# The first stage of a four-branch layer with two input blocks loaded first and its norm and transposes taken by half blocks

## The chip, the cores and the metric

The kernel runs on one core of a Trainium2 chip. The metric is device time in microseconds (us) for one execution of the whole kernel. Five engines run programs of their own and meet at semaphores: TensorE (PE; its weight loads are PEld), VectorE (DVE), ScalarE (ACT), GpSimd (POOL) and SyncE (SP), which only issues transfers. Each engine takes its instructions in the order in which they stand in its program.

## The reference, cut to what matters

```python
def hybrid_layer(x, norm_g, w_in, ...):
    h = rms_norm(x, norm_g)            # x: (1, 512, 1024)
    proj = h @ w_in                    # w_in: (1024, 11208)
    (a_u, a_v, a_z, b_q, b_c, b_qi, b_ki, b_wi, b_z, c_b, c_c, c_x, c_z,
     d_q, d_k, d_v, d_f, d_z, gates) = jnp.split(proj, points, axis=-1)
    y_a = chunked_spatial_gating(a_u, a_v, ...) * jax.nn.silu(a_z)
    y_b = dsa_attention(b_q, b_c, b_qi, b_ki, b_wi, ...) * jax.nn.silu(b_z)
    y_c = short_gated_conv(c_b, c_c, c_x, conv_w) * jax.nn.silu(c_z)
    y_d = forgetting_attention(d_q, d_k, d_v, d_f, fox_b_f) * jax.nn.silu(d_z)
    branch_d = jnp.einsum('nbsw,nwd->bsnd', jnp.stack([y_a, y_b, y_c, y_d]), w_branch)
    merged = jnp.sum(jax.nn.sigmoid(gates) * branch_d, axis=2)
    return x + merged @ w_out          # then a last rms_norm
```

`rms_norm` divides a row of `x` by the root of its mean square and multiplies it by `norm_g`. Everything else in the layer needs the normed input, and the part at issue here is that norm and the first projection, `d_v` (512 columns of `w_in`).

## The kernel before, in words

Every matmul operand is kept as two parts, a rounded high part and the rest as low part, and a product is three matmuls: high with high, high with low, low with high. ACT writes the high part (L80), DVE the low part (L81); the helper `split` does both.

The first stage works on four blocks t of 128 rows of `x` (`xt`, 128x1024). For a block, `norm_x` squares and sums it on ACT (L223), scales the sum on DVE (`rs_v`, L95), takes the root on POOL (`rs`, L96), and multiplies `xt` by the root and by `gB` on DVE in two halves of 512 columns (`xs`, L228). `gB` is `norm_g` on all partitions: two one-row matmuls (`gp`, L263) spread it, and DVE copies them out (L264). `transposed_x` turns the block on PE, four 128x128 transposes to a half (`pt`, L237), and splits each half into `hh` and `hl`, which hold the normed input, turned, for the whole program. `dv_split(i)` splits a quarter of the `d_v` weights (`dvwh`, `dvwl`), and `dv_product(t, i)` is six matmuls of block t with quarter i into `ps_dv` (L144 to L146). The results of the four blocks are split to `vfh`, `vfl`.

All of this stands under `in_order()`, which ties the instructions of PE, DVE and ACT to the order in which the code gives them. What follows (`vfh`/`vfl`, and the next projections with their weights `rawc`, `rawi`, `raw`) is outside it; a scheduler places it among the first stage's instructions when the program is built. The loads of `x`, `norm_g` and the weights are all issued by SP, in the code's order. The remaining stages (the attention branches with a top-k on DVE, the conv, the gates, the output) are some thirty further projections by `proj_fm` with work of the branches between them.

Below, "pt(t, h)" stands for the four transposes of half h of block t, and "hh(t, h)", "hl(t, h)", "xs(t, h)" for the split and the scaling of that half.

Of the kernel before, what the change touches and what calls it, by code (L numbers as in the profile page):

```python
# [8 lines left out]
F32 = mybir.dt.float32  # L9
F32R = mybir.dt.float32r  # L10
AF = mybir.ActivationFunctionType
ALU = mybir.AluOpType
# [5 lines left out]
P = 128  # L18
S = 512
D = 1024  # L20
W = 512
NT = S // P
NK = D // P
# [10 lines left out]
def hybrid_kernel(ctx: ExitStack, tc, x, norm_g, w_in, gm_ln_g, gm_ln_b, gm_w_s, gm_b_s,  # L34
                  dsa_kv_g, dsa_w_uk, dsa_w_uv, conv_w, fox_b_f, w_branch, w_out, final_g, out):
    nc = tc.nc
# [5 lines left out]
    hh = act.tile([P, NK, S], F32R, name="hh")  # L42
    hl = act.tile([P, NK, S], F32R, name="hl")
# [7 lines left out]
    def big(name, dtype=F32R, shape=(P, 4, 512)):  # L51
        return sb.tile(list(shape), dtype, tag="big", name=name, bufs=8)
# [13 lines left out]
    def small(name, cols=1, bufs=4):  # L66
        return sb.tile([P, cols], F32, tag=name, name=name, bufs=bufs)
# [9 lines left out]
    def split(hi, lo, src, scale=None, eng=nc.vector):  # L77

        if scale is None:
            nc.scalar.activation(hi, src, AF.Copy)  # L80
            eng.tensor_tensor(lo, src, hi.bitcast(F32), op=ALU.subtract)  # L81
        else:
            nc.scalar.activation(hi, src, AF.Copy, scale=scale)
            nc.vector.scalar_tensor_tensor(lo, src, scale, hi.bitcast(F32),
                                           op0=ALU.mult, op1=ALU.subtract)
# [6 lines left out]
    def rsqrt(dst, src, scale, n=1):  # L92

        v = small("rs_v", n) if n == 1 else small("rs_w", n, 1)
        nc.vector.tensor_scalar(v, src, scale, EPS, op0=ALU.mult, op1=ALU.add)  # L95
        nc.gpsimd.tensor_tensor(dst, v, negh[:, 0:n], op=ALU.pow)  # L96
# [46 lines left out]
    def term_tm(ps, ah, al, wh, wl, k):  # L143
        nc.tensor.matmul(ps, ah, wh, start=(k == 0), stop=False)  # L144
        nc.tensor.matmul(ps, ah, wl, start=False, stop=False)  # L145
        nc.tensor.matmul(ps, al, wh, start=False, stop=(k == NK - 1))  # L146
# [34 lines left out]
    gB = big("gB", F32, (P, D))  # L181
# [3 lines left out]
    def load_x(t):  # L185
        nc.sync.dma_start(xts[t // 2][:, t % 2, :], x[t * P:(t + 1) * P, :])
# [3 lines left out]
                          w_in[i * 256:(i + 1) * 256, D_V:D_V + W].rearrange("(k p) c -> p k c", p=P))  # L190

    g1 = big("g1", F32, (1, D))
    load_x(0)
    nc.sync.dma_start(g1, norm_g)
    load_dv(0)
    load_x(1)
    load_dv(1)
    load_dv(2)
    load_dv(3)
# [16 lines left out]
    nc.vector.tensor_copy(up, upf)  # L216


    def norm_x(t):
        xt = xts[t // 2][:, t % 2, :]  # L220
        xs = xs2[t // 2][:, t % 2, :]
        ss = small("ss")
        nc.scalar.activation(xs, xt, AF.Square, accum_out=ss)  # L223
        rs = small("rs")
        rsqrt(rs, ss, 1.0 / D)
        for half in range(2):
            hs = slice(half * 512, half * 512 + 512)
            nc.vector.scalar_tensor_tensor(xs[:, hs], xt[:, hs], rs, gB[:, hs],  # L228
                                           op0=ALU.mult, op1=ALU.mult)
        return xs  # L230

    def transposed_x(t, xs):
        for half in range(2):
            pt = at.tile([P, 4, P], F32, tag="at", name="pt")
            for j in range(4):
                k = half * 4 + j
                nc.tensor.transpose(pt[:, j, :], xs[:, k * P:(k + 1) * P], ident)  # L237
            split(hh[:, half * 4:half * 4 + 4, t * P:(t + 1) * P],
                  hl[:, half * 4:half * 4 + 4, t * P:(t + 1) * P], pt)

    def dv_split(i):
        js = slice((i % 2) * 2, (i % 2) * 2 + 2)
        wh, wl = dvw[i // 2]
        split(wh[:, js, :], wl[:, js, :], dvr[i // 2][:, js, :])

    ps_dv = [mm.tile([P, W], F32, tag="mm", name="ps_dv") for _ in range(NT)]

    def dv_product(t, i):
        ts_ = slice(t * P, (t + 1) * P)
        for k in (2 * i, 2 * i + 1):  # L250
            wh, wl = dvw[k // 4]
            term_tm(ps_dv[t], hh[:, k, ts_], hl[:, k, ts_], wh[:, k % 4, :], wl[:, k % 4, :], k)

    with in_order():

        warm = psum("warm")
        for _ in range(8):
            nc.tensor.transpose(warm[:, 0:P], ident, ident)

        for half in range(2):  # L260
            gs = slice(half * 512, half * 512 + 512)
            gp = psum("gp")
            nc.tensor.matmul(gp, up[0:1, 0:P].bitcast(F32), g1[:, gs], start=True, stop=True)  # L263
            nc.vector.tensor_copy(gB[:, gs], gp)  # L264
        xs = norm_x(0)
        dv_split(0)
        transposed_x(0, xs)
        xs = norm_x(1)
        dv_product(0, 0)
        dv_split(1)  # L270
        transposed_x(1, xs)
        dv_product(0, 1)
        dv_product(1, 0)
        dv_product(1, 1)
        dv_split(2)
        xs = norm_x(2)
        dv_split(3)
        dv_product(0, 2)
        dv_product(1, 2)
        transposed_x(2, xs)  # L280
        xs = norm_x(3)
        dv_product(0, 3)
        dv_product(1, 3)
        dv_product(2, 0)
        dv_product(2, 1)
        transposed_x(3, xs)
        dv_product(2, 2)
        dv_product(2, 3)
        for i in range(4):
            dv_product(3, i)  # L290
    vfh, vfl = pair("vf")
    for t in range(NT):
        split(vfh[:, t, :], vfl[:, t, :], ps_dv[t])
# [301 lines left out]
    for t in range(NT):  # L595
# [9 lines left out]
        rs = small("rs")  # L605
# [264 lines left out]
```

## Time and profile before

| | |
|---|---|
| three runs | 709.07, 710.71, 711.07 us (median 710.71) |
| profiled execution, its own time | 711.89 us |
| its span in the trace | 710.2 us |
| PE busy | 693.9 us |
| DVE busy | 364.5 us |
| ACT busy | 275.1 us |

The span runs from the first to the last instruction of the trace; the execution's own time is 1.7 us longer. In a row of the timeline stand the start, the duration, the engine, the line, the operation and its tiles, the count of instructions merged in it, and in brackets how long the engine was idle before it and what ended the wait. A matmul's duration includes its way through the array, so successive matmuls overlap; the distance of their starts is what one costs.

### The profile page before, as it was taken

What the parts mean: (1) busy time and instruction counts of PE and PEld (TensorE: products, weight loads), DVE (VectorE), ACT (ScalarE), POOL (GpSimd) and SP (SyncE); (2) the same over time, 40 slices, a digit from 0 to 9 for tenths busy, and PEclk for the clock granted to TensorE, in tenths of its full rate; (3) what the DMA queues carried; (4) which work ended last, traced back from release to release, by engine and by line L of the source; (5) the groups of instructions that cost most, each with busy time, mean ns of one, the idle gap of its engine ahead of it and who ended that gap; (6) DMA issues with size and microseconds to landing.
All of it is one profiled execution on the core that took longest, in us unless ns stands there. A gap on an engine that the chain in (4) does not pass through costs nothing.

```text
span 710.2 us, 8000 instructions
## 1 busy us (share of the span) xinstructions
PE 693.9 (98%) x3139; PEld 566.4 (80%) x3139; DVE 364.5 (51%) x638; ACT 275.1 (39%) x439; POOL 169.9 (24%) x110
## 2 busy tenths in 40 slices
PE   7999999988999999999999999999999999999996
PEld 4878767766888888888888888888888888888885
DVE  5825699999953664634233343323522334343454
ACT  4616354354444556433322242223322223333233
POOL 1000487341333323203000021222211132111101
PEclk9999999999999999999999999999999999999999
DMA  6715031312112111242322331322313313133233
GB/s 237 219 64 153 4 118 59 112 59 69 60 60 90 60 60 60 61 147 73 105 83 96 118 114 65 119 77 102 120 60 118 117 61 119 60 118 119 62 117 119
DMA packets 56817, 68.05 MB, mean 96 GB/s; under 512 B 3582, under 2 KB 45067, under 8 KB 56780
## 3 DMA queue, kind: packets, MB, share of 16 engines
q1 hardware_dynamic: 55900, 65.46, 28.3%
q0 software_dynamic: 304, 1.05, 0.4%
q10 hardware_dynamic: 576, 1.05, 0.4%
q8 instruction: 24, 0.39, 0.2%
q14 instruction: 13, 0.11, 0.0%
HBM read 64.80 MB, written 2.10 MB: 94 GB/s over the span
## 4 chain that ended last, share of the span: by engine, by line
PE 85%; DVE 11%; DMA 2%; issue 1%; ACT 0%; SPq 0%; POOLq 0%; POOL 0%; DVEq 0%
PE ps_fm L119 18%; PE ps_fm L120 18%; PE ps_fm L124 18%; PE pb L744 4%; PE pb L745 4%; PE pb L747 4%; DVE sc L474 3%; DVE m L473 2%; PE ps_o L144 2%; PE ps_o L146 2%; PE ps_o L145 2%; DVE sc L466 1%; PE pt_ps L533 1%; PE ps_dv L144 1%; DVE l L511 1%
## 5 line engine op out<-in xcount | busy, mean ns | idle before, releaser
L119 PE MATMUL ps_fm<-hh,wh 128*128 128x512 f32 (+1 forms) x640 | 251.3, 393 | 0.0
L120 PE MATMUL ps_fm<-hl,wh 128*128 128x512 f32 (+1 forms) x640 | 250.0, 391 | 0.0
L124 PE MATMUL ps_fm<-hh,wl 128*128 128x512 f32 (+1 forms) x640 | 162.5, 391 | 0.0
L119 PEld LDWEIGHTS ps_fm<-hh,wh 128*128 128x128 f32 (+1 forms) x640 | 120.1, 188 | 26.0 <-issue 0.9
L120 PEld LDWEIGHTS ps_fm<-hl,wh 128*128 128x128 f32 (+1 forms) x640 | 120.0, 187 | 24.9 <-issue 0.2
L124 PEld LDWEIGHTS ps_fm<-hh,wl 128*128 128x128 f32 (+1 forms) x640 | 119.0, 187 | 25.0 <-issue 0.2
L80 ACT ACTIVATE wh<-raw 128x1024 fp32r<-128x1024 f32 x78 | 82.3, 1056 | 114.1 <-PE ps_fm L120 85.0
L81 DVE TENSOR_TENSOR wl<-raw,wh 128x1024 fp32r<-128x1024 f32 x50 | 61.0, 1222 | 78.4 <-PE ps_fm L124 67.1
L81 POOL TENSOR_TENSOR wl<-raw,wh 128x1024 fp32r<-128x1024 f32 x28 | 69.1, 2474 | 111.9 <-PE ps_fm L124 49.2
L753 POOL TENSOR_TENSOR acc<-acc,sg 128x512 f32<-128x512 f32 x24 | 41.8, 1742 | 155.9 <-DVE sg L752 155.9
L744 PE MATMUL pb<-yh,wh 128*128 128x512 f32 x128 | 49.8, 389 | 0.0
L745 PE MATMUL pb<-yl,wh 128*128 128x512 f32 x128 | 49.8, 389 | 0.0
L81 DVE TENSOR_TENSOR wl<-rawb,wh 128x1024 fp32r<-128x1024 f32 x16 | 19.6, 1225 | 51.3 <-PE ps_fm L124 36.8
L80 ACT ACTIVATE wh<-rawb 128x1024 fp32r<-128x1024 f32 x16 | 16.9, 1057 | 50.6 <-PE ps_fm L120 50.6
L752 DVE TENSOR_TENSOR sg<-pb,sg 128x512 f32<-128x512 f32 x24 | 16.6, 692 | 36.3 <-PE pb L747 36.3
L747 PE MATMUL pb<-yh,wl 128*128 128x512 f32 x128 | 34.2, 389 | 0.0
L519 ACT ACTIVATE l<-l,nm 128x128 f32<-128x128 f32 (+3 forms) x32 | 17.9, 560 | 28.5 <-DVE nm L517 28.5
L771 ACT ACTIVATE sg<-ps_fm 128x512 f32<-128x512 f32 x32 | 19.2, 600 | 24.4 <-PE ps_fm L124 24.4
L747 PEld LDWEIGHTS pb<-yh,wl 128*128 128x128 f32 x128 | 24.0, 188 | 5.0
L744 PEld LDWEIGHTS pb<-yh,wh 128*128 128x128 f32 x128 | 24.0, 188 | 5.0
L745 PEld LDWEIGHTS pb<-yl,wh 128*128 128x128 f32 x128 | 24.0, 188 | 5.0
L145 PE MATMUL ps_o<-wl,mh 128*128 128x512 f32 (+1 forms) x72 | 26.2, 366 | 0.0
(242 smaller groups left out, 913.9 us busy)
## 6 DMA issues: line engine op xcount, KB each, us to landing
raw<-in_w_in_dram SPq DMA_DIRECT2D x39, 1024.0 KB, 4.9
rawb<-in_w_branch_dram SPq DMA_DIRECT2D x8, 1024.0 KB, 4.9
rawt<-in_w_out_dram SPq DMA_DIRECT2D x4, 1024.0 KB, 4.9
xt<-in_x_dram SPq DMA_DIRECT2D x4, 512.0 KB, 8.3
rawt<-in_w_in_dram SPq DMA_DIRECT2D x4, 512.0 KB, 8.4
rawt<-in_w_in_dram SPq DMA_DIRECT2D x2, 1024.0 KB, 5.7
xr<-in_x_dram SPq DMA_DIRECT2D x2, 1024.0 KB, 4.9
out_dram<-o SPq DMA_DIRECT2D x4, 256.0 KB, 2.1
```

What stands on the lines that cost most here:

```text
L80: nc.scalar.activation(hi, src, AF.Copy)
L81: eng.tensor_tensor(lo, src, hi.bitcast(F32), op=ALU.subtract)
L119: nc.tensor.matmul(ps[:m], wh[:, k, :], hh[:, k, :], start=(k == 0), stop=False)
L120: nc.tensor.matmul(ps[:m], wh[:, k, :], hl[:, k, :], start=False, stop=False)
L124: nc.tensor.matmul(ps[:m], wl[:, k, :], hh[:, k, :], start=False, stop=(k == NK - 1))
L144: nc.tensor.matmul(ps, ah, wh, start=(k == 0), stop=False)
L145: nc.tensor.matmul(ps, ah, wl, start=False, stop=False)
L474: nc.vector.match_replace(out=scs[i], in_to_replace=m8, in_values=scs[i], imm_value=TAKEN)
L744: nc.tensor.matmul(pb, bh[:, k, cs_], yh[:, k, :], start=(k == 0), stop=False)
L745: nc.tensor.matmul(pb, bh[:, k, cs_], yl[:, k, :], start=False, stop=False)
L747: nc.tensor.matmul(pb, bl[:, k, cs_], yh[:, k, :], start=False, stop=(k == NH - 1))
L753: nc.gpsimd.tensor_tensor(acc, acc, sg, op=ALU.add)
```

## The change

The load of `norm_g` moves from SP to ACT's queue, ahead of everything on ACT. On SP the first two blocks of `x` come first, then the four quarters of the `d_v` weights, then blocks 2 and 3. The eight transposes on `ident` at the start (`warm`) go; three 512-column matmuls on `up` (`keep_warm(3)`) are put between block 0 and block 1. The norm is cut into `square`, `root` and `scaled` (a half), the turn into `transposed_x` (a half) and `parts_x` (the high or the low part of a half), and all are called in a new order. A product takes the high weights of its two k first and the low weights last.

```diff
     g1 = big("g1", F32, (1, D))
+    nc.scalar.dma_start(g1, norm_g)
     load_x(0)
-    nc.sync.dma_start(g1, norm_g)
+    load_x(1)
     load_dv(0)
-    load_x(1)
     load_dv(1)
...
-    def norm_x(t):
...
+    def square(t):
+        sums[t] = small("ss")
+        nc.scalar.activation(xs2[t // 2][:, t % 2, :], xts[t // 2][:, t % 2, :], AF.Square,
+                             accum_out=sums[t])
+
+    def root(t):
+        roots[t] = small("rs")
+        rsqrt(roots[t], sums[t], 1.0 / D)
+
+    def scaled(t, half):
+        hs = slice(half * 512, half * 512 + 512)
+        nc.vector.scalar_tensor_tensor(xs2[t // 2][:, t % 2, hs], xts[t // 2][:, t % 2, hs], roots[t],
+                                       gB[:, hs], op0=ALU.mult, op1=ALU.mult)
...
+    def transposed_x(t, half):
         xs = xs2[t // 2][:, t % 2, :]
...
+        pt = at.tile([P, 4, P], F32, tag="at", name="pt")
+        for j in range(4):
+            k = half * 4 + j
+            nc.tensor.transpose(pt[:, j, :], xs[:, k * P:(k + 1) * P], ident)
+        pts_x[t, half] = pt
+
+    def parts_x(t, half, part):
+        hi = hh[:, half * 4:half * 4 + 4, t * P:(t + 1) * P]
+        lo = hl[:, half * 4:half * 4 + 4, t * P:(t + 1) * P]
+        if part == 0:
+            nc.scalar.activation(hi, pts_x[t, half], AF.Copy)
+        else:
+            nc.vector.tensor_tensor(lo, pts_x[t, half], hi.bitcast(F32), op=ALU.subtract)
...
-            term_tm(ps_dv[t], hh[:, k, ts_], hl[:, k, ts_], wh[:, k % 4, :], wl[:, k % 4, :], k)
+            nc.tensor.matmul(ps_dv[t], hh[:, k, ts_], wh[:, k % 4, :], start=(k == 0), stop=False)
+            nc.tensor.matmul(ps_dv[t], hl[:, k, ts_], wh[:, k % 4, :], start=False, stop=False)
+        for k in (2 * i, 2 * i + 1):
+            wh, wl = dvw[k // 4]
+            nc.tensor.matmul(ps_dv[t], hh[:, k, ts_], wl[:, k % 4, :], start=False,
+                             stop=(k == NK - 1))
 
     with in_order():
 
         warm = psum("warm")
-        for _ in range(8):
-            nc.tensor.transpose(warm[:, 0:P], ident, ident)
-
+
+        def keep_warm(n):
+            for _ in range(n):
+                nc.tensor.matmul(warm, up[:, 0:P], up, start=True, stop=True)
...
+        square(0)
+        root(0)
+        square(1)
+        for half in range(2):
+            nc.vector.tensor_copy(gB[:, half * 512:half * 512 + 512], gps[half])
+            scaled(0, half)
+            transposed_x(0, half)
+            parts_x(0, half, 0)
+        root(1)
+        parts_x(0, 0, 1)
+        parts_x(0, 1, 1)
+        keep_warm(3)
+        dv_split(0, 0)
+        for half in range(2):
+            scaled(1, half)
+            transposed_x(1, half)
+            parts_x(1, half, 0)
+        dv_split(0, 1)
         dv_product(0, 0)
...
+        parts_x(1, 0, 1)
+        parts_x(1, 1, 1)
         dv_product(1, 0)
...
+        for i in range(1, 4):
+            dv_split(i, 0)
+            dv_split(i, 1)
+            dv_product(0, i)
+            dv_product(1, i)
+            if i > 1:
+                square(i)
+                root(i)
+        for t in (2, 3):
+            for half in range(2):
+                scaled(t, half)
+                transposed_x(t, half)
+                parts_x(t, half, 0)
+                parts_x(t, half, 1)
+            for i in range(4):
+                dv_product(t, i)
```

From the third projection on, the five programs stand in the same order as before, but for one 13-column transposition and its copy. The places that moved follow; lines in rows of the changed kernel are its own: L232 is `scaled`, L242 the transposes, L249 and L251 the two parts of a half, L257 and L259 those of the weights, L294 the copy of `gB`.

On DVE at the start of the program, before:

```order
L264 COPY gB<-gp 128x512 x2
L95 TENSOR_SCALAR rs_v<-ss 128x1
L228 SCALAR_TENSOR_TENSOR xs<-xt,rs,gB 128x512 x2
L81 TENSOR_TENSOR dvwl<-rawt,dvwh 128x1024
L81 TENSOR_TENSOR hl<-pt,hh 128x4x128 x2
L95 TENSOR_SCALAR rs_v<-ss 128x1
L228 SCALAR_TENSOR_TENSOR xs<-xt,rs,gB 128x512 x2
```

The same place in DVE's program now:

```order
L95 TENSOR_SCALAR rs_v<-ss 128x1
L294 COPY gB<-gp 128x512
L232 SCALAR_TENSOR_TENSOR xs<-xt,rs,gB 128x512
L294 COPY gB<-gp 128x512
L232 SCALAR_TENSOR_TENSOR xs<-xt,rs,gB 128x512
L95 TENSOR_SCALAR rs_v<-ss 128x1
L251 TENSOR_TENSOR hl<-pt,hh 128x4x128 x2
L232 SCALAR_TENSOR_TENSOR xs<-xt,rs,gB 128x512 x2
L259 TENSOR_TENSOR dvwl<-rawt,dvwh 128x1024
```

The first half of block 0 is scaled as soon as the first half of `gB` is copied, and the scaling of block 1 stands behind the low parts of block 0 but no longer behind `dvwl`.

On DVE where blocks 2 and 3 are scaled, before:

```order
L228 SCALAR_TENSOR_TENSOR xs<-xt,rs,gB 128x512 x2
L81 TENSOR_TENSOR dvwl<-rawt,dvwh 128x1024
L81 TENSOR_TENSOR wl<-rawc,wh 128x1024
L81 TENSOR_TENSOR hl<-pt,hh 128x4x128 x2
L95 TENSOR_SCALAR rs_v<-ss 128x1
L81 TENSOR_TENSOR vfl<-ps_dv,vfh 128x512
L228 SCALAR_TENSOR_TENSOR xs<-xt,rs,gB 128x512 x2
L81 TENSOR_TENSOR wl<-rawi,wh 128x576
L81 TENSOR_TENSOR vfl<-ps_dv,vfh 128x512
L81 TENSOR_TENSOR wl<-raw,wh 128x1024 x2
L81 TENSOR_TENSOR hl<-pt,hh 128x4x128 x2
```

The same place on DVE now:

```order
L232 SCALAR_TENSOR_TENSOR xs<-xt,rs,gB 128x512
L81 TENSOR_TENSOR wl<-rawc,wh 128x1024
L81 TENSOR_TENSOR wl<-rawi,wh 128x576
L81 TENSOR_TENSOR vfl<-ps_dv,vfh 128x512 x2
L251 TENSOR_TENSOR hl<-pt,hh 128x4x128
L232 SCALAR_TENSOR_TENSOR xs<-xt,rs,gB 128x512
L81 TENSOR_TENSOR wl<-raw,wh 128x1024 x2
L251 TENSOR_TENSOR hl<-pt,hh 128x4x128
L232 SCALAR_TENSOR_TENSOR xs<-xt,rs,gB 128x512
L81 TENSOR_TENSOR vfl<-ps_dv,vfh 128x512
L251 TENSOR_TENSOR hl<-pt,hh 128x4x128
L232 SCALAR_TENSOR_TENSOR xs<-xt,rs,gB 128x512
```

Both halves of a block used to be scaled in one go; now the scaling of a block's second half stands behind the low part of its first half, for block 2 and for block 3.

On ACT at the same place, before:

```order
L80 ACTIVATE wh<-rawc 128x1024
L80 ACTIVATE hh<-pt 128x4x128 x2
L223 ACTIVATE xs,ss<-xt 128x1024
L80 ACTIVATE vfh<-ps_dv 128x512
L80 ACTIVATE wh<-rawi 128x576
L80 ACTIVATE vfh<-ps_dv 128x512
L80 ACTIVATE wh<-raw 128x1024 x2
L80 ACTIVATE hh<-pt 128x4x128 x2
L80 ACTIVATE vfh<-ps_dv 128x512 x2
```

And now:

```order
L80 ACTIVATE wh<-rawc 128x1024
L80 ACTIVATE wh<-rawi 128x576
L80 ACTIVATE vfh<-ps_dv 128x512 x2
L249 ACTIVATE hh<-pt 128x4x128
L80 ACTIVATE wh<-raw 128x1024 x2
L249 ACTIVATE hh<-pt 128x4x128
L80 ACTIVATE vfh<-ps_dv 128x512
L249 ACTIVATE hh<-pt 128x4x128 x2
L80 ACTIVATE vfh<-ps_dv 128x512
```

The high part of block 2's first half stands behind `vfh` of blocks 0 and 1, that of its second half behind two weight parts of `raw`, and block 3's first half behind `vfh` of block 2. On PE both halves' transposes of a block still stand together ahead of the block's products.

## Rows read from the trace of the kernel before

**Rows 1.** The page: busy time of the engines, share of the span, instructions.

```profile
PE 693.9 (98%) x3139; PEld 566.4 (80%) x3139; DVE 364.5 (51%) x638; ACT 275.1 (39%) x439; POOL 169.9 (24%) x110
```

**Rows 2.** The page: the chain that ended last, by engine.

```profile
PE 85%; DVE 11%; DMA 2%; issue 1%; ACT 0%; SPq 0%; POOLq 0%; POOL 0%; DVEq 0%
```

**Rows 3.** Waits of PE, 0 to 60 us: us in total, times, longest.

```profile
PE pt L237 <- DVE xs L228: 3.0, 2, 2.4
```

**Rows 4.** Timeline of PE, 0 to 20 us.

```profile
4.22 3.75 PE L263 MATMUL gp<-g,up 1*128 1x512 f32 x4 [0.27 <-DMA g<-in_norm_g_dram]
10.33 1.94 PE L237 MATMUL pt<-ident,xs 128*128 128x128 f32 x8 [2.36 <-DVE xs L228]
...
15.69 1.94 PE L237 MATMUL pt<-ident,xs 128*128 128x128 f32 x8 [0.66 <-DVE xs L228]
17.28 0.77 PE L144 MATMUL ps_dv<-dvwh,hh 128*128 128x512 f32 x1
...
18.28 0.63 PE L146 MATMUL ps_dv<-dvwh,hl 128*128 128x512 f32 x1
18.71 0.63 PE L144 MATMUL ps_dv<-dvwh,hh 128*128 128x512 f32 x1
...
19.66 0.40 PE L144 MATMUL ps_dv<-dvwh,hh 128*128 128x512 f32 x1
19.89 0.39 PE L145 MATMUL ps_dv<-dvwl,hh 128*128 128x512 f32 x1
```

**Rows 5.** Timeline of ACT and DVE in the same stretch.

```profile
2.79 0.43 DVE L216 CAST up<-upf 128x512 fp32r<-128x512 f32 x1 [1.87 <-POOL upf L214]
...
4.12 1.06 ACT L223 ACTIVATE xs<-xt 128x1024 f32<-128x1024 f32 x1 [2.04 <-DMA xt<-in_x_dram]
...
8.00 0.69 DVE L264 COPY gB<-gp 128x512 f32<-128x512 f32 x1 [1.01 <-PE gp L263]
...
9.43 1.41 DVE L228 SCALAR_TENSOR_TENSOR xs<-xt,rs,gB 128x512 f32<-128x512 f32 x2 [0.67 <-POOL rs L96]
...
11.45 0.60 ACT L80 ACTIVATE hh<-pt 128x512 fp32r<-128x512 f32 x1 [3.05 <-PE pt L237]
12.08 0.69 DVE L81 TENSOR_TENSOR hl<-pt,hh 128x512 fp32r<-128x512 f32 x1
...
12.80 1.05 ACT L223 ACTIVATE xs<-xt 128x1024 f32<-128x1024 f32 x1
```

**Rows 6.** Issues of SP: two of the first, and one block's time to landing.

```profile
0.80 0.38 SPq L186 DMA_DIRECT2D xt<-in_x_dram  x1
1.24 0.30 SPq L194 DMA_DIRECT2D g<-in_norm_g_dram  x1
...
xt<-in_x_dram SPq DMA_DIRECT2D x1, 512.0 KB, 6.6
```

**Rows 7.** Timeline of all engines, 24 to 36 us.

```profile
25.14 1.03 PE L237 MATMUL pt<-ident,xs 128*128 128x128 f32 x8
25.77 1.09 ACT L80 ACTIVATE hh<-pt 128x512 fp32r<-128x512 f32 x2 [3.63 <-PE pt L237]
...
26.40 1.29 DVE L81 TENSOR_TENSOR hl<-pt,hh 128x512 fp32r<-128x512 f32 x2 [1.53 <-ACT hh L80]
...
30.91 2.01 ACT L80 ACTIVATE wh<-raw 128x1024 fp32r<-128x1024 f32 x2 [1.35 <-DMA raw<-in_w_in_dram]
...
34.87 0.39 PE L146 MATMUL ps_dv<-dvwh,hl 128*128 128x512 f32 x1
...
35.29 0.60 ACT L80 ACTIVATE vfh<-ps_dv 128x512 fp32r<-128x512 f32 x1 [1.40 <-PE ps_dv L146]
...
35.92 0.69 DVE L81 TENSOR_TENSOR vfl<-ps_dv,vfh 128x512 fp32r<-128x512 f32 x1 [0.28 <-ACT vfh L80]
```

**Rows 8.** Stretches in mid-kernel: length, busy time by engine, granted clock (PEclk), DMA.

```profile
166.00:169.30 3.30, 1.44 (x5) 0.84 (x6) 3.30 (x10) 3.07 (x7) 1.61 (x1) 1.00 0.00 0
169.30:172.70 3.40, 3.40 (x16) 3.30 (x15) 3.40 (x10) 2.22 (x7) 0.77 (x1) 0.52 0.44 135
```

More of the change, by code (lines that the diff above doesn't have):

```diff
@@ L216, in hybrid_kernel @@
     nc.vector.tensor_copy(up, upf)
-    def norm_x(t):
-        xt = xts[t // 2][:, t % 2, :]
-        xs = xs2[t // 2][:, t % 2, :]
[L222 to L241, printed above, removed]
+    sums, roots = {}, {}
+    def square(t):
+        sums[t] = small("ss")
+        nc.scalar.activation(xs2[t // 2][:, t % 2, :], xts[t // 2][:, t % 2, :], AF.Square,
+                             accum_out=sums[t])
@@ new lines, in root @@
+    def root(t):
[5 more added lines that the diff above has]
+                                       gB[:, hs], op0=ALU.mult, op1=ALU.mult)
+    pts_x = {}
+    def transposed_x(t, half):
+        xs = xs2[t // 2][:, t % 2, :]
+        pt = at.tile([P, 4, P], F32, tag="at", name="pt")
[3 more added lines that the diff above has]
+        pts_x[t, half] = pt
@@ L242, in dv_split @@
+    def parts_x(t, half, part):
[5 more added lines that the diff above has]
+            nc.vector.tensor_tensor(lo, pts_x[t, half], hi.bitcast(F32), op=ALU.subtract)
+    def dv_split(i, part):
         js = slice((i % 2) * 2, (i % 2) * 2 + 2)
         wh, wl = dvw[i // 2]
-        split(wh[:, js, :], wl[:, js, :], dvr[i // 2][:, js, :])
+        if part == 0:
+            nc.scalar.activation(wh[:, js, :], dvr[i // 2][:, js, :], AF.Copy)
+        else:
+            nc.vector.tensor_tensor(wl[:, js, :], dvr[i // 2][:, js, :], wh[:, js, :].bitcast(F32),
+                                    op=ALU.subtract)
@@ L254, in hybrid_kernel @@
     with in_order():
         warm = psum("warm")
-        for _ in range(8):
-            nc.tensor.transpose(warm[:, 0:P], ident, ident)
+        def keep_warm(n):
+            for _ in range(n):
+                nc.tensor.matmul(warm, up[:, 0:P], up, start=True, stop=True)
+        gps = []
         for half in range(2):
-            gs = slice(half * 512, half * 512 + 512)
             gp = psum("gp")
-            nc.tensor.matmul(gp, up[0:1, 0:P].bitcast(F32), g1[:, gs], start=True, stop=True)
-            nc.vector.tensor_copy(gB[:, gs], gp)
@@ L265, in hybrid_kernel @@
[L265 to L268, printed above, removed]
+            nc.tensor.matmul(gp, up[0:1, 0:P].bitcast(F32), g1[:, half * 512:half * 512 + 512],
+                             start=True, stop=True)
+            gps.append(gp)
+        square(0)
[6 more added lines that the diff above has]
+            parts_x(0, half, 0)
@@ L269, in hybrid_kernel @@
+        root(1)
[8 more added lines that the diff above has]
+        dv_split(0, 1)
         dv_product(0, 0)
-        dv_split(1)
-        transposed_x(1, xs)
-        dv_product(0, 1)
+        parts_x(1, 0, 1)
+        parts_x(1, 1, 1)
         dv_product(1, 0)
-        dv_product(1, 1)
-        dv_split(2)
-        xs = norm_x(2)
@@ L277, in hybrid_kernel @@
[L277 to L290, printed above, removed]
+        for i in range(1, 4):
[6 more added lines that the diff above has]
+                root(i)
```

## The prediction

> **What bounds the kernel now.** I read the page's busy times first: PE is busy for 693.9 us, 98% of the span [rows 1]. The chain that ended last agrees: 85% of it runs on PE and 11% on DVE, the latter in the top-k of mid-kernel [rows 2]. That top-k starts on matmuls of PE, so what the first stage loses or gains is passed on one for one to the end; nothing later has slack that would take it up. I therefore look only at what PE does before the third projection.
>
> The waits there: PE waits for the scaled halves `xs` twice, 3.0 us in all [rows 3]. The timeline of PE has them at 10.33 and 15.69; from 15.69 to 60 us, PE waits for nothing more [rows 3, 4]. Second, the clock. Starts of 512-column matmuls are 0.43 us apart at 18.28 and 18.71 and 0.23 apart at 19.66 and 19.89 [rows 4]: the lower of the two levels (1.2 GHz) until about 19.2, the upper (2.4 GHz) after. While it lasts, every microsecond costs (0.43 - 0.23)/0.43 = 0.47 us.
>
> **The change, part by part.** All times are on the clock of the trace before.
>
> *The head up to the first product.* A common mark is "blocks 0 and 1 turned and `dv_product(0, 0)` issued", which PE reaches at 17.28 now [rows 4]. I rebuild it link by link. `square(0)` starts at 4.12 as before and is done before `gB`. The second copy of `gB` starts at 8.00 and takes 0.69 [rows 5]; the sum, the root and the first half of block 0 lie beside the two `gp` matmuls. So xs(0, 1) starts at 8.69. From the start of a scaling to the start of its transposes it is 10.33 - 9.43 = 0.90 [rows 4, 5], so pt(0, 1) starts at 9.59. From there to hh it is 11.45 - 10.33 = 1.12, and from hh to hl 0.63 [rows 4, 5]: hl(0, 1) at 11.34. One DVE instruction later (0.69) xs(1, 0) starts at 12.03, and pt(1, 0) at 12.93. Eight transposes take PE 17.28 - 15.69 = 1.59 [rows 4], so the product starts at 14.52 and, at the slow pace, is issued at 14.52 + 6 x 0.43 = 17.1. Gain: 0.2 us, with `norm_g` landing as late as now.
>
> `norm_g` is the other half of it: PE waited for it until 4.22 [rows 4]. It was issued at 1.24, behind a block issued at 0.80 [rows 6]; as the first thing on ACT it goes out 0.44 sooner. Bounds: no gain, and 0.9 (the wait would then end near 3.3, when the other operand, `up`, is made [rows 5]). I take the 0.44 of the issue. Head: **-0.7**, between -0.2 and -1.1.
>
> *Blocks loaded first.* The second block landed 6.6 us after an issue near 2.0 [rows 6], that is at about 8.6, and was first read at 12.80 [rows 5]: its load was never waited for. Having it sooner is worth nothing by itself, and nothing is charged for the weights behind it, since `dvwh` is read only after hh(0, 1), past 11. But `square(1)` now stands on ACT ahead of hh(0, 0); were block 1 to land after about 7.9, the head would move with it. Sent as second transfer I expect it near 7, so 0.
>
> *Warm-up.* The eight transposes lie before `norm_g` lands, and the three matmuls of `keep_warm` (1.3 us) lie in the gap between pt(0, 1) and pt(1, 0). Cost 0. The clock may rise sooner: PE's unbroken run starts at 12.5 to 12.9 instead of 15.69. If the rise follows the run's start by as much as now (19.2 - 15.69 = 3.5), it comes 2.8 to 3.2 us sooner and saves up to 1.5; if it stays at 19.2, nothing. Nothing in the trace prefers one end; I take the middle, **-0.7**.
>
> *Blocks 2 and 3: a new wait.* Now PE turns block 2 without a gap: eight transposes in 1.03 at 25.14 [rows 7]. In the changed order xs(t, 1) stands behind hl(t, 0) on DVE, hl(t, 0) needs hh(t, 0), and that needs pt(t, 0) on PE; pt(t, 1) stands on PE ahead of all of the block's products. So between the two halves PE has nothing that it may issue. Let pt(2, 0) start at T, directly behind `dv_product(1, 3)`. The last `vfh` ahead of hh(2, 0) waits for that product: 35.29 - 34.87 = 0.42 after its last matmul's start, that is T + 0.19 [rows 7]. Two such ACT pieces run 1.09 in all [rows 7], so hh(2, 0) ends at T + 1.3. On DVE `vfl` starts 0.63 behind `vfh` [rows 7], T + 0.82, and hl(2, 0) follows 0.6 to 0.65 later (1.29 for two of them [rows 7]), T + 1.45; xs(2, 1) starts at T + 2.05, and pt(2, 1) at T + 2.95 by the same 0.90. PE itself worked 0.52 of it. A gap of **2.4 us**. Block 3 has the same chain, with `vfh` of block 2 ahead. Sum **+4.8**. Lower bound: without `vfh` and `vfl` in the way 0.6 less in each, 3.6. Upper bound: hh(2, 1) also stands behind two `wh<-raw` of 2.01 in all, which waited for their load until 30.91 [rows 7]; if that load comes no sooner than now, `dv_product(2, 2)` waits some 1.5 us. Its buffer comes free sooner in the new order, so I take 0 for it.
>
> *The clock in these gaps.* Mid-kernel there is a stretch of 3.30 us in which PE was busy for 1.44, in pieces; in the 3.40 us behind it the granted clock was 0.52 [rows 8], the lower level. A gap of 2.4 us, with PE busy on both sides, is of that kind. A fall costs 3.4 x 0.47 = 1.6. Bounds: none, or one for each gap, 3.2. I take one, **+1.6**, since a gap can lie so that no stretch is as idle as that one.
>
> The Trainium skill ("TensorE: Matmul & The Clock Gate", section "Why this matters for your kernels") speaks only against idle gaps longer than either of these; by that rule neither gap brings the clock down, and the sum would be 1.6 less. The trace does not bear this out fully, since the stretch at 166 us held no single wait as long as 2.4 us and was still followed by the lower clock.
>
> *Products with low weights last.* The same six matmuls; DVE has `dvwl` ready in time now (PE waits on nothing but `xs` [rows 3]), so 0.
>
> **Sum.** -0.7 - 0.7 + 4.8 + 1.6 = **+5.0 us**. The profiled execution took 711.89 (span 710.2 and 1.7 around it) and would become 716.9. It lies 1.2 above the median of the three runs, 710.7, which I take as the base: **715.7 us**.
>
> **The rivals.** A change below 0.3% (2.1 us, about the spread of the three runs) cannot be told from none.
>
> *No fall of the clock.* Both gaps, but the lower clock follows neither: 710.7 + 3.4 = 714.1. This is what the skill's rule gives. For it: no gap alone is as long as the rule names; against it, rows 8.
>
> *Two falls.* 710.7 + 6.6 = 717.3. For it: both gaps are alike, and the stretches around them are mostly idle.
>
> *Not slower: a readier clock.* If the clock rises already in the work on block 0, and stays up in the gaps, then PE runs at the upper level when the products start at 14.1. It saves 0.47 x (19.2 - 14.1) = 2.4 and some 0.4 on the last transposes, 2.8 in place of 0.7: 710.7 - 0.7 - 2.8 + 4.8 = 712.0, no difference that can be told. It decides if the rise comes before about 14.6 us and no fall follows. Against it: PE was busy nearly without pause through `gp` from 4.22 for 3.75 us and the clock was still low at 18.71 [rows 4].
>
> *The change gives nothing at its head.* With `norm_g` no sooner and the clock rising at 19.2, 1.2 of the gains go: 716.9. That is inside the range.
>
> **How the numbers follow.** Forecast (two gaps, one fall) 0.45; no fall 0.18; two falls 0.20; readier clock 0.08; anything that removes the gaps or pays for them elsewhere 0.09. The likeliest gives 715.7. The range takes in the no-fall case with the best head (714.1 - 1.2 = 712.9, and a little of the readier clock) and two falls with a poor head (717.3 + 1.2 = 718.5): 712.4 to 718.6. Slower by over 0.3% hold the first three and a part of the fourth, 0.85; same 0.11; faster 0.04.
>
> **What would show it.** In the waits of PE, two rows of transposes on DVE's `xs` of some 2.4 us each, near 27 to 30 and 35 to 39 us, each ahead of block 2's and block 3's second half. `dv_product(0, 0)` issued by about 16.6 to 17.1. A granted clock of about half in a few microseconds behind a gap, and matmul starts 0.23 apart earlier than 19.2. Wrong I would be if PE ran through blocks 2 and 3 without a gap, or if mid-kernel waits on DVE shrank by as much as the first stage lost.

## The result, and the profile after

The changed kernel takes 715.08 us (median of 5 runs, 712.43 to 715.52) where the kernel before took 710.71 on the same chip (5 runs, 709.07 to 711.99): a ratio of 1.0056 (95% interval 1.0032 to 1.0081), 4.4 us slower. In a second timing the same kernel stood at 715.5 against 711.2 (1.0069, 1.0049 to 1.0089).

The profiled execution of the changed kernel is its fastest, 712.43 us with a span of 710.7. First the busy times on its page, then the waits of PE from 0 to 60 us:

```profile
PE 691.7 (97%) x3134; PEld 565.2 (80%) x3134; DVE 362.4 (51%) x638; ACT 275.5 (39%) x439; POOL 170.4 (24%) x110
```

```profile
PE pt L242 <- DVE xs L232: 5.4, 3, 2.3
PE gp L287 <- DVE up L216: 3.3, 1, 3.3
```

Where PE had waited 3.0 us for `xs` in all [rows 3], it now waits 5.4, and it no longer waits for `norm_g` but for `up`, the other operand of `gp`. The 3.3 us of that wait are no loss: nothing stands ahead of `gp` on PE any more, and `gp` starts at 3.28 instead of 4.22. The timeline of PE shows where (number in brackets: the wait ahead and what ended it):

```profile
3.28 3.77 PE L287 MATMUL gp<-g,up 1*128 1x512 f32 x4 [3.28 <-DVE up L216]
7.12 1.08 PE L242 MATMUL pt<-ident,xs 128*128 128x128 f32 x4
8.62 1.11 PE L242 MATMUL pt<-ident,xs 128*128 128x128 f32 x4 [0.42 <-DVE rs_v L95]
9.39 1.63 PE L281 MATMUL warm<-up 128*128 128x512 f32 x3
11.90 1.94 PE L242 MATMUL pt<-ident,xs 128*128 128x128 f32 x8 [0.89 <-DVE xs L232]
...
16.20 0.63 PE L268 MATMUL ps_dv<-dvwh,hh 128*128 128x512 f32 x1
16.63 0.45 PE L269 MATMUL ps_dv<-dvwh,hl 128*128 128x512 f32 x1
16.92 0.40 PE L268 MATMUL ps_dv<-dvwh,hh 128*128 128x512 f32 x1
17.15 0.40 PE L269 MATMUL ps_dv<-dvwh,hl 128*128 128x512 f32 x1
...
28.86 0.66 PE L242 MATMUL pt<-ident,xs 128*128 128x128 f32 x4 [2.23 <-DVE xs L232]
...
37.75 0.63 PE L242 MATMUL pt<-ident,xs 128*128 128x128 f32 x4 [2.32 <-DVE xs L232]
```

The mark "`dv_product(0, 0)` issued" stands at 16.20 where it stood at 17.28 [rows 4]: 1.08 gained. Starts are 0.43 apart up to 16.63 and 0.23 after 16.92, so the clock rises near 16.75 and not near 19.2 [rows 4]. This is read from the distances of the starts alone: the column of the granted clock has 1.00 from 12.00 to 20.00 us in both profiles. Ahead of the second halves of blocks 2 and 3 stand the two new waits, 2.23 and 2.32.

What lies in the first of these gaps, on DVE and ACT (block 3's is alike):

```profile
26.23 0.60 ACT L80 ACTIVATE vfh<-ps_dv 128x512 fp32r<-128x512 f32 x1 [0.77 <-PE ps_dv L272]
26.72 0.59 ACT L249 ACTIVATE hh<-pt 128x512 fp32r<-128x512 f32 x1
26.86 0.69 DVE L81 TENSOR_TENSOR vfl<-ps_dv,vfh 128x512 fp32r<-128x512 f32 x1 [0.68 <-ACT vfh L80]
27.47 0.68 DVE L251 TENSOR_TENSOR hl<-pt,hh 128x512 fp32r<-128x512 f32 x1
27.55 2.01 ACT L80 ACTIVATE wh<-raw 128x1024 fp32r<-128x1024 f32 x2 [0.24 <-DMA raw<-in_w_in_dram]
28.06 0.74 DVE L232 SCALAR_TENSOR_TENSOR xs<-xt,rs,gB 128x512 f32<-128x512 f32 x1
```

This is the chain of the prediction, link by link: `vfh` and `hh` on ACT, `vfl` and `hl` on DVE, and only then the second half of `xs`.

Yet this execution is only 0.5 us longer in its span than the one before (710.7 against 710.2). At a row that both have, the second of four pieces of `val` on DVE (low parts of an operand of the first branch), the changed kernel is 2.72 us late; then it catches up. Here that row, a row of PE at the end of the top-k (`po`, the first matmul that waits for the low part `ptl`), and what happens between them; before:

```profile
91.29 2.15 DVE L81 TENSOR_TENSOR val<-vn,vah 128x512 fp32r<-128x512 f32 x1
...
157.20 2.39 POOL L81 TENSOR_TENSOR wl<-raw,wh 128x1024 fp32r<-128x1024 f32 x1 [1.20 <-ACT pth L80]
157.76 1.97 DVE L511 TENSOR_TENSOR l<-l,causal 128x128 f32<-128x128 f32 x1
...
168.69 0.50 PE L89 MATMUL po<-ptl,vfh 128*128 128x512 f32 x1 [1.48 <-DVE ptl L81]
```

and in the changed kernel:

```profile
94.01 2.14 DVE L81 TENSOR_TENSOR val<-vn,vah 128x512 fp32r<-128x512 f32 x1
...
160.48 0.26 DVE L548 TENSOR_TENSOR l<-l,causal 128x128 f32<-128x128 f32 x1
161.51 2.40 POOL L81 TENSOR_TENSOR wl<-raw,wh 128x1024 fp32r<-128x1024 f32 x1 [2.79 <-ACT pth L80]
...
169.98 0.50 PE L89 MATMUL po<-ptl,vfh 128*128 128x512 f32 x1 [1.10 <-DVE ptl L81]
```

From `val` to `po` it was 77.40 and is 75.97, 1.43 less. One small DVE piece (the causal mask added to attention logits) is enough to explain it: before, it starts while GpSimd (POOL) runs a 2.39 us subtraction and ends only with it (1.97 us); in the changed kernel that GpSimd piece comes later, and the same DVE piece takes 0.26, 1.71 less. From `po` to the end of the span it was 541.5 and is 540.7: the fall of the clock [rows 8] stood behind `po`, on PE's own path; now it stands at 153.2 to 156.5, where DVE is the bound (length, busy time of PE, PEld, DVE, ACT and POOL, granted clock, DMA):

```profile
153.20:156.50 3.30, 3.30 (x10) 2.56 (x9) 3.30 (x10) 2.54 (x5) 0.19 (x1) 0.51 0.02 5
```

That the later start of the GpSimd piece comes from this fall (it waits for `pth`, a link behind PE's matmuls) is read from its releaser, not tried by itself. The account of the span: +2.72 - 1.43 - 0.8 = +0.5.

### The profile page after: what moved, and what is told of

Its sections match the earlier page's. It is cut to its first block, busy times and chain, and to the rows that moved or that the text cites. A ratio compares the mean times of both kernels' runs of the same rounds, so it can differ in the third digit from the quotient of the medians.

```text
span 710.7 us, 7990 instructions
## 1 busy us (share of the span) xinstructions
PE 691.7 (97%) x3134; PEld 565.2 (80%) x3134; DVE 362.4 (51%) x638; ACT 275.5 (39%) x439; POOL 170.4 (24%) x110
## 4 chain that ended last, share of the span: by engine, by line
PE 85%; DVE 12%; issue 1%; ACT 1%; POOL 0%; POOLq 0%; DVEq 0%
PE ps_fm L119 18%; PE ps_fm L124 18%; PE ps_fm L120 18%; PE pb L784 4%; PE pb L782 4%; PE pb L781 4%; DVE sc L511 3%; DVE m L510 3%; PE ps_o L146 2%; PE ps_o L145 2%; PE ps_o L144 2%; DVE sc L503 1%; PE ps_dv L268 1%; PE pt_ps L570 1%; PE ps_dv L272 1%
## 5 line engine op out<-in xcount | busy, mean ns | idle before, releaser
L81 POOL TENSOR_TENSOR wl<-raw,wh 128x1024 fp32r<-128x1024 f32 x28 | 69.2, 2477 | 109.7 <-PE ps_fm L124 49.2
L789 DVE TENSOR_TENSOR sg<-pb,sg 128x512 f32<-128x512 f32 x24 | 16.6, 691 | 36.3 <-PE pb L784 36.3
L808 ACT ACTIVATE sg<-ps_fm 128x512 f32<-128x512 f32 x32 | 19.2, 600 | 24.6 <-PE ps_fm L124 24.6
L556 ACT ACTIVATE l<-l,nm 128x128 f32<-128x128 f32 (+3 forms) x32 | 17.9, 560 | 25.4 <-DVE nm L554 25.3
```

## The experiments

Times within one group are compared with the kernel before on the same chip.

**First group (before: 711.2).** *r0_changed_again* is the changed kernel itself.

> The changed kernel as it stands. Theory (two gaps, and the lower clock behind them in most executions): median near 715.1, executions at about 712.4 where the clock stays up behind both gaps and near 715.5 where it falls behind them; waits of PE on the scaled halves of blocks 2 and 3 of 2.2 to 2.3 us each in every execution. Rival (the loss comes in mid-kernel, by where the one fall there lies): the spread of single times is not tied to the mean granted clock.

Measured: 715.5 (715.01 to 716.47), ratio 1.0069 (1.0049 to 1.0089). All six executions lie on the upper of the two expected levels, none near 712.4; and the slowest of them has the highest mean granted clock (716.47 at 0.994), so the mean clock alone does not put them in order, as the rival said. The profiled execution (715.64) is an ordinary one. The gaps are the same, 2.24 and 2.33, but after the second the clock is low, as its stretches show (length, busy time by engine, granted clock):

```profile
35.00:38.00 3.00, 0.72 (x6) 0.39 (x4) 1.95 (x3) 1.08 (x2) 0.00 (x0) 0.97 0.55 210
38.00:41.20 3.20, 3.15 (x10) 2.70 (x11) 0.69 (x1) 0.60 (x1) 0.00 (x0) 0.50 0.00 0
41.20:45.00 3.80, 3.80 (x18) 3.13 (x17) 0.00 (x0) 0.00 (x0) 0.00 (x0) 1.00 0.00 0
```

In the faster execution above, the same place behind an equally idle stretch (PE busy 0.68 of 3.00) shows no fall:

```profile
38.00:41.00 3.00, 3.00 (x17) 2.50 (x16) 0.69 (x1) 0.60 (x1) 0.00 (x0) 1.00 0.00 0
```

Against it, r0's `val` row comes 1.81 later (95.82). Of that, 0.30 is there already at the second gap (38.05 against 37.75 for the transposes behind it), so the fall cost 1.51. Against the kernel before, r0 is 4.53 late at `val`, 4.55 at `po` and 3.7 at the end of the span (713.9).

*e1_both_halves_scaled_first*: only the scalings of blocks 2 and 3 are taken ahead of the first transposes.

```
         for t in (2, 3):
             for half in range(2):
                 scaled(t, half)
+            for half in range(2):
                 transposed_x(t, half)
```

> Blocks 2 and 3 scale both halves before the first transposes, nothing else undone. Theory: the two gaps go (4.6 us), and no clock falls in the first stage; the third projection starts near 50.1 instead of 54.7 and the kernel takes 709.0 (707.5 to 710.2), below the kernel before. Rival (mid-kernel gives the lost time back, so the gaps cost less than they measure): 710.5 to 712.5.

Measured: 710.0 (708.88 to 710.91), ratio 0.9988 (0.9974 to 1.0002): 5.5 below the changed kernel and within the expected range; that it is below the kernel before, as expected, is not shown, since the interval takes in 1. No wait between halves is left; the eight transposes run in one group, and what follows on PE is

```profile
26.11 1.04 PE L242 MATMUL pt<-ident,xs 128*128 128x128 f32 x8
27.45 0.50 PE L268 MATMUL ps_dv<-dvwh,hh 128*128 128x512 f32 x1 [0.30 <-ACT hh L249]
28.28 0.50 PE L269 MATMUL ps_dv<-dvwh,hl 128*128 128x512 f32 x1 [0.33 <-DVE hl L251]
```

Two small waits for the parts remain, since block 2's own products now stand directly behind its transposes; the kernel before had other products there.

*e2_only_the_new_wait* is the reverse: the kernel before, with the second half of each of blocks 2 and 3 scaled between the halves' transposes and nothing else of the change.

```
-        for half in range(2):
+        def scaled(half):
             hs = slice(half * 512, half * 512 + 512)
...
+        scaled(0)
+        if t < 2:
+            scaled(1)
+        late[t] = scaled
         return xs
+
+    late = {}
 
     def transposed_x(t, xs):
         for half in range(2):
+            if half == 1 and t > 1:
+                late[t](1)
```

> The kernel before, with only the scaling of the second half of blocks 2 and 3 put behind the low part of the first half. Theory: PE waits some 1.7 us in block 2 (no vfh in the way there) and 2.0 to 2.3 us in block 3, and the head is that of before; 714.4 with no fall of the clock, up to 717 with falls. Rival (the loss of the changed kernel comes from its head or its weight order): within 1 us of the kernel before.

Measured: 716.29 (713.23 to 717.83), ratio 1.0073 (1.0048 to 1.0097). The wait alone costs 5.1, as much as the whole change (4.3) within the noise. The gap of block 2 was expected at 1.7 and is 2.16, as that of block 3. Here the clock falls behind both (granted clock 0.50 from 27.7 to 31.0 and from 37.9 to 41.2):

```profile
24.50:27.70 3.20, 1.13 (x7) 1.07 (x8) 2.10 (x3) 1.69 (x3) 0.00 (x0) 0.99 1.07 298
27.70:31.00 3.30, 3.30 (x9) 2.52 (x8) 1.90 (x4) 2.85 (x6) 0.55 (x1) 0.50 0.93 299
```

*e3_gaps_filled* leaves the gaps but has nine extra matmuls, whose result nothing reads, between the halves of blocks 2 and 3.

```
                 parts_x(t, half, 0)
                 parts_x(t, half, 1)
+                if half == 0:
+                    keep_warm(9)
```

> The changed kernel with nine 512-column matmuls on a spare operand between the two halves' transposes of blocks 2 and 3 (extra work that no output uses). The order of the other engines stays, so the second half's transposes come as late as before, but PE is busy. Theory (the clock falls behind the gaps): the gaps' 4.6 us stay, the falls go: 712.2 in all executions (711.5 to 713). Rival (no falls of the clock in the median, other delays): 715, as the changed kernel.

Measured: 713.01 (712.03 to 715.12), ratio 1.0034 (1.002 to 1.0049), 2.5 below the changed kernel. The matmuls take 2.33 and leave waits of 0.24; the mean granted clock of all twelve executions is 0.996 or 0.997, where r0's are 0.990 to 0.994. The expectation had 711.5 to 713 for all executions; the median lies on that edge and 715.12 far above it, at a mean clock of 0.997, so the clock is not all that spreads them. Some 2.5 us of the changed kernel's time go with the clock that the gaps bring down. What is left above the kernel before is 1.8, less than the gaps and the gain at the beginning would make (4.55 - 1.72 = 2.83, worked out below); the difference lies behind the first stage: its profiled execution is 3.34 late at `val` and 1.1 at the end of the span.

**Second group (before: 710.6).** *e8_head_alone* keeps the beginning of the change and puts blocks 2 and 3 back where the kernel before had them (`norm_x` squares and scales both halves of a block, `both` does all its transposes and parts).

```
-        for i in range(1, 4):
...
+        dv_split(2, 0)
+        dv_split(2, 1)
+        norm_x(2)
+        dv_split(3, 0)
+        dv_split(3, 1)
+        dv_product(0, 2)
+        dv_product(1, 2)
+        both(2)
+        norm_x(3)
+        for job in ((0, 3), (1, 3), (2, 0), (2, 1)):
+            dv_product(*job)
+        both(3)
+        for job in ((2, 2), (2, 3), (3, 0), (3, 1), (3, 2), (3, 3)):
+            dv_product(*job)
```

> The change's beginning with the work of blocks 2 and 3 put back where the kernel before had it: both halves of block 2 scaled right behind the split of weight piece 2 and transposed in one group after the products (0,2) and (1,2); block 3 scaled behind that and transposed after (2,1). Nothing is left out. Theory (the beginning gains 1.08 at the mark 'product(0,0) issued' and 0.67 by the earlier clock rise, and the gaps of blocks 2 and 3 cost everything that the change lost): no gap between the halves and none of the 0.3 us waits for parts that the kernel with both halves scaled first had; 709.2 us (707.8 to 710.2), 6 below the changed kernel, and 0.8 below the kernel with both halves scaled first. Rival 1 (the start of a beginning is not passed on, the first stage is bound by something later): 711.0, as before the change. Rival 2 (the 0.3 us waits cost nothing): 710.0, as with both halves scaled first.

Measured: 707.48 (705.76 to 710.51), ratio 0.9963 (0.9944 to 0.9981), a version faster than both kernels and below the expected range. Its transposes stand at 23.01 and 29.37 without a wait, and `val` at 89.15, 2.14 ahead of the kernel before. The executions lie on two levels, nine from 705.8 to 707.9 and three from 709.9 to 710.5. The profiled one (span 705.9) has no long DVE piece beside GpSimd behind 145 us, and gains 1.4 between `val` and `po` and 0.8 behind it, as above: 2.14 + 1.4 + 0.8 = 4.3, its span against 710.2.

*e9_head_dv0_second*, *e10_head_g_on_sync* and *e11_head_no_keep_warm* each undo one thing in e8_head_alone:

```
     load_x(0)
-    load_x(1)
     load_dv(0)
+    load_x(1)
```

> The kernel of e8_head_alone with the loads in the old interleaving: x block 0, weight piece 0, x block 1, weight piece 1 (norm_g stays on ScalarE's queue). Nothing is left out. The prediction's term (the order of the blocks and the weights is worth nothing): the mark 'product(0,0) issued' stays at 16.2 and the time at 709.2 (707.8 to 710.2). Rival: the square of block 1 stands ahead of the first copy of block 0's high parts on ScalarE, and block 1 comes about 2 us later (512 KB at some 260 GB/s, landing 7.4 instead of under 5.4), so that copy starts at 8.6 instead of 8.24 and the mark moves to 16.6: 709.6.

Measured: 707.31 (705.2 to 710.09), ratio 0.9957 (0.9939 to 0.9975). The square of block 1 now waits for its load until 7.78 (5.74 in e8) and holds the first `hh` to 8.84 (8.53), but block 1's transposes start at 12.06 against 11.98. The order of blocks and weights is worth nothing that can be measured.

```
-    nc.scalar.dma_start(g1, norm_g)
     load_x(0)
+    nc.sync.dma_start(g1, norm_g)
```

> The kernel of e8_head_alone with norm_g issued on SyncE's queue behind x block 0, as in the kernel before, in place of ScalarE's. Nothing is left out. Theory (the early norm_g is what the beginning gains): the four gp matmuls start at 4.2 instead of 3.28, the first copy of gB ends at 6.3 and the first scaling starts at 7.0 instead of 6.22, the mark 'product(0,0) issued' comes at 17.0 instead of 16.2, 710.0 us (708.6 to 711.0). Rival: the half-block chain of transposes and copies gives the gain by itself and the first scaling hardly waits for gB: mark at 16.2 to 16.5, 709.3.

Measured: 708.21 (706.92 to 711.34), ratio 0.9981 (0.9962 to 1.0001), 0.73 above e8; the two spreads overlap widely, so the place in the trace weighs more. `gp` starts at 4.16, block 1's transposes at 12.75 instead of 11.98. In this profile, though, the clock had risen by 13.8, before the first product, so its span (705.2) shows no loss: the rise is not at the same place in each execution.

```
-        keep_warm(3)
```

> The kernel of e8_head_alone without the three extra matmuls (9.39 to 11.0) whose result nothing reads. No work of the reference is left out. The prediction's term (they cost and give nothing): nothing waits for them, the clock rises at 16.6 to 16.9 as with them, 709.2 us (707.8 to 710.2). Rival: TensorE's idle stretch from 9.7 to 11.9 puts the rise off by up to the 3 us that the kernel before had it later (19.7), the matmuls in that stretch start 0.43 apart instead of 0.23, so up to 1.4 us more: 710.6.

Measured: 709.9 (707.4 to 710.54), ratio 0.9979 (0.996 to 0.9999), 2.4 above e8, and so against the expectation. But block 1's transposes start at 11.90 and the clock rises near 16.6, where it rose near 16.0 in e8 and near 16.75 in the changed kernel with the matmuls. The executions lie on the same two levels, four at 707.4 to 707.5 and six at 709.9 to 710.5. The profiled one is of the upper: the DVE piece takes 1.94 beside a GpSimd piece of 2.38, and the clock falls behind `po`. From this I put the two levels down to the meeting of DVE and GpSimd, and the next group takes the meeting away.

**Third group (before: 710.7), and a fourth (711.0).** In all four kernels each of GpSimd's 28 subtractions of 128x1024 is cut into four:

```
-            eng.tensor_tensor(lo, src, hi.bitcast(F32), op=ALU.subtract)
+            if eng is nc.gpsimd:
+                for q in range(4):
+                    qs = slice(2 * q, 2 * q + 2)
+                    eng.tensor_tensor(lo[:, qs, :], src[:, qs, :], hi[:, qs, :].bitcast(F32), op=ALU.subtract)
+            else:
+                eng.tensor_tensor(lo, src, hi.bitcast(F32), op=ALU.subtract)
```

*e12_pool_split_in_four* does it to e8_head_alone, *e13_pool_four_no_warm* also drops `keep_warm(3)`; *e14_before_pool_four* does it to the kernel before and *e15_after_pool_four* to the changed kernel.

> The kernel of e8_head_alone in which each of the 28 subtractions of 128x1024 that GpSimd does for the weights' low parts (2.4 us each) is written as four of 128x256. Nothing is left out. Theory (the two levels of its executions, 707.4 and some 710, come from one small VectorE piece that meets such a GpSimd piece and ends only with it, 0.26 becoming 1.97 in the kernel before): with pieces of some 0.6 to 0.8 us on GpSimd no VectorE piece of 0.26 us lasts longer than about 0.9, the level of 710 is gone or within 1 us of the other, and the median is 707.0 (705.8 to 708.5). Rival 1 (the length of the GpSimd piece does not matter, the two engines slow each other as long as both work): the VectorE piece lasts 1.9 us in spite of the pieces, two levels 2.4 us apart as before. Rival 2 (four starts on GpSimd instead of one make the weights late): GpSimd's busy time goes up by over 28 x 1 us and the time by several us.

Measured: 704.5 (703.23 to 705.21), ratio 0.9918 (0.9903 to 0.9933), 3.0 below e8 and more than expected. None of the six executions is on an upper level. Groups of instructions (form, busy us, mean ns), first e8, then e12:

```profile
L81 POOL TENSOR_TENSOR wl<-raw,wh 128x1024 fp32r<-128x1024 f32 x28 | 69.2, 2478 | 109.7 <-PE ps_fm L124 49.2 <-ACT wh L80 35.6 <-ACT l L573 5.3
...
L562 DVE TENSOR_TENSOR l<-l,causal 128x128 f32<-128x128 f32 x16 | 8.3, 523 | 0.1
L81 DVE TENSOR_TENSOR val<-vn,vah 128x512 fp32r<-128x512 f32 x4 | 7.2, 1810 | 0.1
```

```profile
L84 POOL TENSOR_TENSOR wl<-raw,wh 128x256 fp32r<-128x256 f32 x112 | 85.4, 794 | 97.1 <-PE ps_fm L129 39.8 <-ACT l L578 16.9 <-ACT pth L80 9.6
...
L567 DVE TENSOR_TENSOR l<-l,causal 128x128 f32<-128x128 f32 x16 | 5.8, 372 | 0.1
L86 DVE TENSOR_TENSOR val<-vn,vah 128x512 fp32r<-128x512 f32 x4 | 3.2, 807 | 0.1
```

GpSimd works 16 us longer on the subtractions, and DVE as a whole 10.9 less (362.3 to 351.4 on the pages): it met GpSimd at more places than the one that I had named. That was the size that my expectation missed. Another way to gain would be weights that are ready sooner for PE, piece by piece; but PE waits for none of these subtractions in the profiles of the kernel before, e8, e12 and e14. What goes with the cutting is two waits of PE for DVE, there in the kernel before and gone in e14 (as they are in e8, the second with 1.1, and gone in e12):

```profile
PE nb_ps L440 <- DVE rl L84: 1.5, 1, 1.5
PE po L89 <- DVE ptl L81: 1.5, 1, 1.5
```

> The kernel of e12_pool_split_in_four without the three extra matmuls at the beginning, whose result nothing reads. No work of the reference is left out. Theory (the three matmuls are worth nothing, and the 2.4 us between the medians with and without them came from the share of executions on the upper of two levels): the same time as e12_pool_split_in_four within 0.5 us. Rival (the three matmuls keep the clock's state such that a later fall lies where it costs nothing): slower than that kernel by 1 to 2.5 us.

Measured: 703.87 (703.43 to 704.31), ratio 0.9909 (0.9894 to 0.9925), 0.6 from e12 and not slower. The three matmuls are worth nothing that can be measured; this bears out that the 2.4 us of e11 came from its share of executions on the upper level.

> The kernel before with GpSimd's subtractions for the weights' low parts in four pieces of 128x256, as in e12_pool_split_in_four, and nothing of the change. Nothing is left out. Theory (the beginning of the change is worth 1.1 at the mark and 0.7 by the earlier clock rise, and without the chance meetings of VectorE and GpSimd it arrives at the end whole): 1.8 above e12_pool_split_in_four, 706.3 us (705.3 to 707.3). Rival (part of what the beginning seemed to give was the other level of the middle stretch): under 0.8 above, 705.0.

> The changed kernel with GpSimd's subtractions for the weights' low parts in four pieces of 128x256, as in e12_pool_split_in_four. Nothing is left out. Theory (the prediction's sum, with nothing given back or lost later): the kernel of e14_before_pool_four plus 4.55 for the two gaps, less 1.8 for the beginning, plus 1.8 for one fall of the clock in most executions: 710.9 us (709 to 711.5). Rival (the fall was brought by the meetings or costs nothing on the path): 709.1.

Measured: e14 705.35 (704.5 to 706.29), ratio 0.9935 (0.9918 to 0.9952); e15 710.32 (708.37 to 711.34), ratio 0.9999 (0.9986 to 1.0012). The change costs 4.97 here, and e15 lies within its expected range. The cutting alone takes 5.6 off the kernel before. e14 is 0.85 above e12, between theory and rival, but on another chip (0.54 when each is taken against its own kernel before). In the profiles it is 1.48 behind at `val` (89.98 against 88.50) and gains 1.4 behind `po`, where e12 has a fall of the clock and e14 has none. The stretch of the top-k, 96 to 160 us, shows what the cutting did; before, e14, e15:

```profile
96.00:160.00 64.00, 62.19 (x260) 46.76 (x260) 63.86 (x148) 27.87 (x46) 33.84 (x17) 1.00 0.30 98
```

```profile
96.00:160.00 64.00, 64.00 (x275) 49.03 (x275) 62.35 (x168) 28.85 (x48) 39.99 (x51) 1.00 0.32 99
```

```profile
96.00:160.00 64.00, 64.00 (x268) 48.29 (x267) 61.27 (x162) 29.65 (x47) 43.83 (x54) 1.00 0.32 99
```

The first two numbers behind the length are PE's and PEld's busy time, the third is DVE's. Before, DVE was busy for 63.86 of the 64 us and PE was idle for 1.81; now PE is busy all the time. In e12, e13, e14 and e15 alike it is 73.3 us from `val` to the `po` row that was used above. With PE busy throughout, this stretch gives nothing back and takes nothing: e15 is 4.81 behind e14 at `val`, 4.81 at `po` and 4.6 at the end of the span.

## Why the prediction was right, point by point

The sum of +5.0 stands beside +4.4 and +4.3 measured in the two timings, and beside +4.97 where DVE and GpSimd no longer meet (e15 against e14). Its terms:

*Head (-0.7, bounds -0.2 and -1.1): -1.08.* The mechanism was right and the upper bound the size: I gave `norm_g` the 0.44 of its earlier issue, and PE waits for `up` instead, so it had landed by 3.28. e10 prices that part at 0.77 on PE, which leaves some 0.3 for the half blocks (0.2 worked out).

*Earlier clock (-0.7): -0.64.* PE stays at the slow pace for 0.55 behind the mark instead of 1.92, and 0.47 of that is saved. That the size fits is luck: the place of the rise varies between executions, from before 12.94 in e15 to near 17.9 in e13. The first stage of e15 is that of the changed kernel, and it reaches block 2 at 23.93 instead of 26.03, 2.1 sooner by the clock alone.

*Loads and `keep_warm` (0): 0*, by e9 and e13. `square(1)` started at 5.43 without a wait.

*Two gaps of 2.4 (+4.8): 2.23 + 2.32 = +4.55.* e1 takes them away and is 5.5 below the changed kernel; e2 brings them alone and is 5.1 above the kernel before. The upper bound (the loads of `raw` that `wh` waits for) did not come up: that wait is 0.24 in the profile. At `val` the terms so far make -1.08 - 0.64 + 4.55 = 2.83, and 2.72 was measured.

*One fall of the clock (+1.6): from none to two.* A fall cost 1.51 (r0). The fastest execution shows none in the first stage and is, by that stage alone, the rival "no fall"; e3 puts what the falls cost in an ordinary execution at 2.5, between my one and two. The Trainium skill ("TensorE: Matmul & The Clock Gate", section "Why this matters for your kernels") speaks only against idle gaps longer than these. By the runs that is no safe limit: gaps of 2.16 and 2.33 were followed by the low clock in e2 and r0, while in the profile of the changed kernel gaps of 2.23 and 2.32 were not; in e15 gaps of the same 2.23 and 2.32 were both followed by it (granted clock 0.60 from 28 to 32 us, 0.82 from 40 to 44).

*"Passed on one for one; nothing later has slack": wrong.* This step failed. In the kernel before and in the changed kernel the top-k is bound by DVE, and from `val` to `po` it takes one of two lengths in the ten profiles with uncut subtractions: 75.95 to 76.02 in seven, 77.37 to 77.42 in three, where one more small piece meets GpSimd's subtraction (before, e11 and r0). The clock falls inside the stretch in the seven and in r0, and about `po` or behind it in before and e11. r0 with the fall and before without it are equally long (77.42, 77.40), so the fall costs nothing there; behind `po` it costs 0.8. So a profiled execution could show +0.5. That the shift at the beginning decides which of these an execution gets is likely, but was not tried by itself. It is only with the meetings removed (e14, e15) that the first stage is passed on nearly whole in the profiles, as the prediction had it. The medians came out at +4.4 all the same, and in part by luck: with 2.5 for the falls the measured terms make +5.3, and some 1.0 of it is taken back behind the first stage, where the prediction had nothing. That both kernels have executions with and without such a meeting would explain it (the kernel before spreads over 708.4 to 712.7 in 35 runs), but this is not shown.

What stays open: which share of executions gets which level, and why. Only profiled executions show the cause, and there are one or two for each kernel.

## What to carry to other kernels

When work is cut into halves to start earlier, see what stands between the halves on the engine that consumes them: at the beginning PE had nothing else to do and the cut gained 1.1 us, in the middle of a stream of products it opened two gaps of 2.3 us. Scale or copy all halves before the first is consumed, and put other products behind the transposes (e8, 3.1 us faster than the kernel before; with GpSimd's pieces cut in both, 0.5 to 0.9 of that is left, e12 against e14). Before trusting a difference of a few us, look for long GpSimd pieces beside DVE's; cutting them in four was worth 3.0 on e8 (e12) and 5.6 on the kernel before (e14), more than the order of the first stage.

## What the runs showed of the hardware

Some DVE instructions that start while GpSimd runs a subtraction on SBUF end only with that one: `l<-l,causal` takes 1.97 us from 157.76 in the kernel before, beside GpSimd's 157.20 to 159.59, and 0.26 alone; in r0 it was a piece of `sc<-sc`, 2.00 beside 2.40. The Trainium skill ("SBUF — State Buffer", section "Who interferes with whom") says that the two engines share a pair of ports and that the second waits for the whole instruction of the first; the trace agrees, and e12 shows what follows from it: four pieces of 0.79 cost GpSimd more (85.4 against 69.2 us) and the kernel less.

A low clock need not make an execution slower. In the profiles of the changed kernel and of e8 it falls inside the DVE-bound stretch, the GpSimd piece starts later, and the execution is 1.4 us shorter there than those of the kernel before and of e11, in which the clock held past 166 us [rows 8]. It is no rule: in r0 the clock fell there too, and GpSimd's piece met another piece of DVE's instead.
